# Decay and rate up-projections of a hybrid RWKV-7 / HGRN-2 layer: two products on 128 rows in place of three on 64

## The chip, the cores and the metric

The kernel runs on one core of a Trainium2 chip, as one launch. Its time is the device time in microseconds (us). Before the change it is 3080.24 us, the median of three runs (3078.0 to 3082.81). The engines are PE (matrix products, with weight loads, PEld, beside them), DVE (VectorE), ACT (ScalarE), POOL (GpSimd) and SP, which only issues DMAs. Each takes its own instructions in the order of the program.

## The reference

One layer on x [2048, 1024]. A projection u = x @ w_in feeds two branches. What the change touches is in the first:

```
u = u + (token_shift(u) - u) * mu
xw = u[..., C_WD:C_AD]        # 64 inputs of the decay
xa = u[..., C_AD:C_GD]        # 64 inputs of the rate
w_log = -softplus(-(w0 + tanh(xw) @ w_up)) - 0.5      # w_up [64, 512]
decay = exp(-exp(w_log))
a = sigmoid(a0 + xa @ a_up)                           # a_up [64, 512]
g = sigmoid(xg) @ g_up                                # 128 inputs
y = rwkv7_scan(r, decay, k, v, -kk, kk * a)
```

The second branch is a gated recurrence in chunks (HGRN-2, 4 heads). Both go through gates and an output matrix, then follow a layer norm, a routed mixture of 32 experts, a second layer norm and a gate on a side input. All of it is in float32.

## The kernel before

**Precision.** Products in the type fp32r are made exact enough by splitting both operands: `split` (lines 66 to 72) writes the high part by an ACT copy and the low part by a DVE subtraction. A product is then high x high, high x low and low x high.

**Phases.** The first phase (`phase_a`, to about 1640 us) computes the projection and both recurrences; then come the output products with gates (names pp, wab, gt), w_o with the first norm and the router, the experts, and the end. The first phase goes over four blocks of 512 tokens. A block has 46 projections `proj(ct)` of 128 columns, each of 24 products (lines 269 to 271: eight parts of the features, three products each), four head pairs of the first branch and four heads of the second. Projection 12 holds the 64 decay inputs on partitions 0 to 63 and the 64 rate inputs on 64 to 127; projection 13 the 128 gate inputs; 0 to 11 r, k and v; 14 to 29 the heads of the second branch; 30 to 45 the gates. `prep` makes projections 12 and 13 and splits their results into lh, ll (decay and rate) and gh, gl (gate).

**The up-projections.** Per head pair (128 of 512 columns) `s1a` calls `lora` twice. With r the rows 0 to 63 for the decay (pw), 64 to 127 for the rate (pa), it issues three products that contract over 64 partitions:

```
PE.matmul(o, wh[r, c], ah[r], start=True, stop=False)     # L333
PE.matmul(o, wh[r, c], al[r], start=False, stop=False)    # L334
PE.matmul(o, wl[r, c], ah[r], start=False, stop=True)     # L335
```

The gate's up-projection (pg) uses the same function with all 128 rows.

**The first branch.** `g1` forms the chunk products (pA, line 420); DVE masks them (A, line 425), and the lower triangles go to DRAM (Lsc) and back (Lt). `inv` inverts 32x32 blocks on DVE in 31 steps (lines 455 and 457), and the result goes through DRAM (Msc) into MI. `g2` makes further operands (pB, pV); `ops` combines (p, line 534); `chain` runs the state through 8 chunks of a head pair (py lines 571 and 572, pt 578, Sbd, ST). `hgrn` is the second branch: levels of masked products (g, line 649; kc, att), then transposes (tk, tv), po and pS.

**What sets the order.** The generators of a block are woven by weights, which gives the program its first order; then the tile framework reorders each engine's instructions by its own timing model (`schedule_with_timeline_sim=True`). So any edit can give another order, on all engines. Tiles lie on two stacks of pools in SBUF, and a later phase's tile waits for the earlier ones in its place. `tt` gives a ring of 4 scratch tiles, weights of a projection a ring of 3.

Of the kernel before, what the change touches and what calls it, by code (L numbers as in the profile page):

```python
# [10 lines left out]
F32 = mybir.dt.float32  # L11
F32R = mybir.dt.float32r
# [10 lines left out]
T = 2048  # L23
# [25 lines left out]
def hybrid_kernel(ctx, tc, x, p, w_in, rw_mu, rw_w0, rw_w_up, rw_a0, rw_a_up, rw_g_up, rw_k_k, rw_k_a,  # L49
# [66 lines left out]
    def phase_a(pool, lpool):  # L116
# [51 lines left out]
        def load_x(b, xh, xl, tags):  # L168
            """x^T of block b, split: a step for each 128 of its features"""
# [53 lines left out]
        plb = cp.tile([128, 4], F32, name="plb")      # lb + (1-lb)/2  # L223
# [10 lines left out]
        hlb = cp.tile([128, 4], F32, name="hlb")      # (1-lb)/2  # L234
# [5 lines left out]
        # loras  # L240
        wua_h = cp.tile([128, 512], F32R, name="wua_h")
        wua_l = cp.tile([128, 512], F32R, name="wua_l")
# [3 lines left out]
        ltmp = tt("ltmp")  # L246
        nc.sync.dma_start(ltmp[0:64], rw_w_up[0])
        nc.sync.dma_start(ltmp[64:128], rw_a_up[0])
        split(wua_h, wua_l, ltmp)
# [31 lines left out]
        def turned2(dst, src, g4):  # L281
            """block-diagonal form of four chunks, columns (half, head, 32), the halves changed over in odd chunks"""
            for h in range(2):
                r = slice(64 * h, 64 * h + 64)
                for u in range(2):
                    i_ = src[r, 4 * g4 + u:4 * g4 + 4:2, :].rearrange("q c (a t) -> q c a t", a=2)
                    yield (dst[r].rearrange("q c (a x t) -> q c a x t", a=2, x=2)[:, u::2, :, h, :],
                           i_[:, :, ::-1, :] if u else i_)
# [3 lines left out]
        def block(b):  # L292
# [19 lines left out]
            def prep():  # L312
                if b == 0:
                    bt["xh"], bt["xl"] = x0
# [1 line left out]
                lh = bt["lh"] = ev.tile([128, 512], F32R, tag="lh", name=f"lh{b}")  # L316
                ll = bt["ll"] = ev.tile([128, 512], F32R, tag="ll", name=f"ll{b}")
# [4 lines left out]
                split(lh, ll, u)  # L322
# [7 lines left out]
            def lora(wh, wl, ah, al, r, hp, name, tag="rw"):  # L330
                o = bank(tag, 2, name)
                c = slice(128 * hp, 128 * hp + 128)
                PE.matmul(o, wh[r, c], ah[r], start=True, stop=False)  # L333
                PE.matmul(o, wh[r, c], al[r], start=False, stop=False)  # L334
                PE.matmul(o, wl[r, c], ah[r], start=False, stop=True)  # L335
                return o

            def rstd_bcast(sq, ones, n, eps, opm, name, tag):
                """[128, 512] of rows' (max(sum, eps) or sum + eps)^-1/2, broadcast over the summed rows, in PSUM."""
# [17 lines left out]
            def s1a(hp, ukv, st):  # L357
# [3 lines left out]
                pw = lora(wua_h, wua_l, bt["lh"], bt["ll"], slice(0, 64), hp, "pw" + n)  # L361
# [16 lines left out]
                pa = lora(wua_h, wua_l, bt["lh"], bt["ll"], slice(64, 128), hp, "pa" + n)  # L378
# [30 lines left out]
            def g1(hp, st):  # L409
                """a^T (b, k, I) of the chunks; L to DRAM"""  # L410
# [21 lines left out]
            def inv(hp, st):  # L432
                """inverse of the 32x32 diagonal blocks of I - L"""
# [8 lines left out]
                # partition (g, blk): row r is row 4r+g of the identity  # L442
# [24 lines left out]
            def g2(hp, st):  # L467
                """b^T, k^T with (r, I); the centred v; block-diagonal forms"""
# [50 lines left out]
            def ops(hp, st):  # L519
                """chunk operators"""  # L520
# [20 lines left out]
                # (I - L)^-1 by halves of 32 tokens: a pair of chunks at a time  # L541
# [23 lines left out]
            def chain(hp, st):  # L565
# [22 lines left out]
                pg = lora(gu_h, gu_l, bt["gh"], bt["gl"], slice(0, 128), hp, "pg" + n, "ch")  # L588
# [6 lines left out]
            def hgrn(h, hook=None):  # L595
# [11 lines left out]
                V.scalar_tensor_tensor(q, q, 1.0, pq, op0=ALU.add, op1=ALU.mult)     # 2 silu(q)  # L607
# [106 lines left out]
            def next_x():  # L714
                """loads x, and has a step of its turn into x^T for each of the last ones of the block before"""
# [31 lines left out]
        cen = cp.tile([128, 128], F32, name="cen")    # I - ones/64 within each head  # L747
# [6 lines left out]
        # tokens of a chunk's a and b on partitions (half, head, 32): the halves change places in odd chunks  # L754
        strictP = cp.tile([128, 2, 64], F32, name="strictP")  # (., parity, s): s < t
        strictH = cp.tile([128, 2, 2, 64], F32, name="strictH")  # the same, one head's rows
        inclP = cp.tile([128, 2, 64], F32, name="inclP")      # (., parity, t): t >= s
        inclT = cp.tile([128, 64], F32, name="inclT")         # partition (h,s), col t: t >= s
# [23 lines left out]
        # HGRN: odd chunks hold k and v backwards, so that a level's earlier halves of an even and of an odd chunk  # L782
        # lie on complementary positions.  Masks: position s, (chunk, later half's t)
        hm = cp.tile([128, 7, 128], U8, name="hm")
        hmf = tt("hmf")[:, 0:128]
        for lv in range(7):
# [3 lines left out]
            for u, sg in ((0, 1), (1, -1)):  # L790
                # keep 2h*b <= s < 2h*b + h, where s is the position or 127 minus it
# [6 lines left out]
        # persistent tiles with fixed zero or identity parts  # L798
# [60 lines left out]
    def ln_rows(pl, s, n, bufs=2):  # L859
        """mean and rstd of the rows of s [128, D] -> (rstd, -mean * rstd)"""  # L860
# [73 lines left out]
    def phase_b2(pool, outp, mg, last):  # L934
# [33 lines left out]
        def first(d, io, oh, name):  # L968
            """one-hot of the first place where d (value minus the maximum) is 0"""
# [8 lines left out]
        def route(b, lg):  # L978
# [32 lines left out]
            # exp(d) = (1 + tanh(d/2)) / (1 - tanh(d/2))  # L1011
# [91 lines left out]
    def pe_setup(hold, tmp):  # L1103
        """p @ w_pe, row tile by row tile, into pe_d: the first NPE tiles wait for the end of the experts"""
# [632 lines left out]
```

## Time and profile before

| | |
|---|---|
| median of three runs | 3080.24 us (3078.0 to 3082.81) |
| span of the profiled execution, its only time | 3081.2 us |
| PE busy | 2993.2 us, 97% |
| PEld busy (beside PE) | 2571.2 us, 83% |
| DVE busy | 2130.2 us, 69% |
| ACT busy | 1554.2 us, 50% |
| POOL busy | 541.5 us, 18% |

The profile is of one execution. Busy times of PE are modelled and overlap by a part of each product, so the step from one start to the next says what a product takes of the stream. The clock of PE has two levels, and a stretch shows their mean (1.00 is full). A row of waits gives who waited, for whom, the us in total, how often, and the longest.

### The profile page before, as it was taken

To read this page: it belongs to the slowest core of one execution; us is meant where nothing else is said; L and a number is where in the kernel's file an instruction comes from. 1 tells how busy PE (TensorE), PEld (TensorE's weight loads), DVE (VectorE), ACT (ScalarE), POOL (GpSimd) and SP (SyncE) were. 2 spreads that over 40 slices of the span, in tenths; PEclk is the share of its full clock that TensorE was granted. 3 is DMA by queue.
4 is the path that set the end of the run, shared out by engine and by line. 5 is a ranking of instruction groups with operands and counts; after the bars stand their busy time and mean duration, and the time that the engine had idled before them with its cause. 6 is when DMAs were issued, how large, how long until landed. Compare 5 with 4: busy or idle time off the path is not lost.

```text
span 3081.2 us, 50028 instructions
## 1 busy us (share of the span) xinstructions
PE 2993.2 (97%) x17080; PEld 2571.2 (83%) x17080; DVE 2130.2 (69%) x4827; ACT 1554.2 (50%) x3119; POOL 541.5 (18%) x827
## 2 busy tenths in 40 slices
PE   8999999999999999999988999998999999999799
PEld 6888888888888888888877999987888888887687
DVE  5777768777777767777678777754545555655785
ACT  5555555555655556555534434333545555555442
POOL 4111112211112111212113011121111111112200
PEclk9999999999999999999999999999999999999899
DMA  4333323333233242323335333239889999996661
GB/s 119 96 88 101 105 76 99 88 87 113 83 95 85 87 119 83 91 81 85 87 100 178 110 101 111 89 130 366 292 294 327 315 333 332 338 337 232 233 225 68
DMA packets 438135, 491.41 MB, mean 159 GB/s; under 512 B 91334, under 2 KB 310470, under 8 KB 437878
## 3 DMA queue, kind: packets, MB, share of 16 engines
q1 hardware_dynamic: 424566, 445.45, 44.9%
q0 software_dynamic: 13312, 42.74, 3.8%
q8 instruction: 136, 2.23, 0.3%
q14 instruction: 121, 0.99, 0.1%
HBM read 417.66 MB, written 70.42 MB: 158 GB/s over the span
## 4 chain that ended last, share of the span: by engine, by line
PE 85%; DVE 6%; DMA 4%; issue 2%; SPq 1%; ACT 1%; POOL 0%; POOLq 0%; DVEq 0%; ACTq 0%
PE pp L269 10%; PE pp L271 10%; PE pp L270 10%; PE py L1339 7%; PE w1p L1394 4%; PE p L534 3%; PE w3p L1394 3%; PE po L1064 2%; PE po L1062 2%; PE po L1063 2%; PE pg L1555 2%; PE pg L1556 2%; PE pp L923 2%; PE pp L922 2%; PE pp L921 2%
## 5 line engine op out<-in xcount | busy, mean ns | idle before, releaser
L69 DVE TENSOR_TENSOR lw<-w,hw 128x1024 fp32r<-128x1024 f32 x256 | 308.9, 1222 | 207.6 <-ACT hw L67 205.6
L67 ACT ACTIVATE hw<-w 128x1024 fp32r<-128x1024 f32 x256 | 267.5, 1056 | 117.1 <-PE py L1339 64.3
L455 DVE TENSOR_TENSOR pr<-M,Lt 128x2 f32<-128x2 f32 (+30 forms) x496 | 169.5, 342 | 35.2 <-POOL Lt L441 24.8
L921 PE MATMUL pp<-yh,wh 128*128 128x256 f32 x512 | 146.5, 287 | 7.2 <-DVE gt L924 7.2
L923 PE MATMUL pp<-yh,wl 128*128 128x256 f32 x512 | 146.2, 286 | 3.7 <-DVE wl L69 3.7
L922 PE MATMUL pp<-yl,wh 128*128 128x256 f32 x512 | 146.9, 288 | 0.0
L1394 PE MATMUL w1p<-xT,w 128*128 128x152 f32 (+5 forms) x1024 | 143.7, 297 | 0.7 <-ACT xT L1311 0.7
L67 ACT ACTIVATE wh<-wab 128x512 fp32r<-128x512 f32 x128 | 80.1, 629 | 123.3 <-PE pp L922 121.2
L1394 PEld LDWEIGHTS w1p<-xT,w 128*128 128x128 f32 x1024 | 139.1, 192 | 2.6 <-ACT xT L1311 0.9
L1394 PE MATMUL w3p<-xT,w 128*128 128x152 f32 (+5 forms) x1024 | 136.3, 294 | 0.0
L1394 PEld LDWEIGHTS w3p<-xT,w 128*128 128x128 f32 x1024 | 134.5, 190 | 0.0
L457 DVE TENSOR_REDUCE M<-pr 128x1 f32<-128x2 f32 (+30 forms) x496 | 126.1, 254 | 10.5
L1351 POOL DMA_INDIRECT ybuf<-y,it x48 | 62.2, 1297 | 297.0 <-ACT y L1349 225.7
L921 PEld LDWEIGHTS pp<-yh,wh 128*128 128x128 f32 x512 | 98.4, 193 | 10.7 <-issue 7.0
L1318 DVE SCALAR_TENSOR_TENSOR u<-t,w3p 128x512 f32<-128x512 f32 (+6 forms) x48 | 26.1, 543 | 113.4 <-PE w3p L1394 83.3
L923 PEld LDWEIGHTS pp<-yh,wl 128*128 128x128 f32 x512 | 98.5, 193 | 6.5 <-DVE wl L69 5.6
L1265 POOL DMA_INDIRECT xg<-x_d,it x48 | 52.4, 1092 | 288.9 <-DMA it<-tokbuf 284.0
L69 DVE TENSOR_TENSOR wl<-wab,wh 128x512 fp32r<-128x512 f32 x124 | 89.4, 722 | 19.7 <-ACT wh L67 18.3
L1339 PE MATMUL py<-hw,hTl 128*128 128x512 f32 x256 | 102.2, 399 | 0.0
L1339 PE MATMUL py<-lw,hTh 128*128 128x512 f32 x256 | 101.8, 397 | 0.0
L1062 PE MATMUL po<-woh,mh 128*128 128x512 f32 x256 | 101.5, 397 | 0.0
L1063 PE MATMUL po<-woh,ml 128*128 128x512 f32 x256 | 101.2, 395 | 0.0
(1044 smaller groups left out, 9422.1 us busy)
## 6 DMA issues: line engine op xcount, KB each, us to landing
w<-in_w_dram SPq DMA_DIRECT2D x384, 512.0 KB
gt_d<-gt SPq DMA_DIRECT2D x64, 256.0 KB
gt<-gt_d SPq DMA_DIRECT2D x64, 256.0 KB
yg<-ybuf SPq DMA_DIRECT2D x32, 512.0 KB
xr<-in_x_dram SPq DMA_DIRECT2D x32, 256.0 KB
Lt<-Lsc SPq DMA_DIRECT2D x64, 128.0 KB
xr<-in_x_dram SPq DMA_DIRECT2D x16, 512.0 KB
x_d<-s SPq DMA_DIRECT2D x16, 512.0 KB
```

The lines of the kernel that those rows point to most:

```text
L67: a = S.activation(hi, src, AF.Copy, **({} if scale is None else {"scale": scale}))
L69: v = (G if pool else V).tensor_tensor(lo, src, hi.bitcast(F32), op=ALU.subtract)
L269: PE.matmul(o, wh[:, i % 4, :], xh, start=(i == 0), stop=False)
L270: PE.matmul(o, wh[:, i % 4, :], xl, start=False, stop=False)
L271: PE.matmul(o, wl[:, i % 4, :], xh, start=False, stop=(i == n - 1))
L455: V.tensor_tensor(pr[:, r0:, 0:w], M[:, r0:, j:32], lt[:, None, :].to_broadcast([128, 8 - r0, w]), op=ALU.mult)
L921: PE.matmul(pp[:, u, :], w[u][0][:, k, :], yh[i], start=(k == 0), stop=False)
L922: PE.matmul(pp[:, u, :], w[u][0][:, k, :], yl[i], start=False, stop=False)
L923: PE.matmul(pp[:, u, :], w[u][1][:, k, :], yh[i], start=False, stop=(k == 3))
L1062: PE.matmul(po, mh[:, tsl], woh[k][:, cs], start=(k == 0), stop=False)
L1339: PE.matmul(py[c][0:n], h[:, j, :], st["w2s", j][w][:, cs], start=(j == 0 and i == 0), stop=(j == 3 and i == len(seq) - 1))
L1394: PE.matmul(ph[nm][j // 2][:, j % 2, 0:cap], st[nm, k // 2][:, k % 2, 128 * j:128 * j + 128], xT[:, k, 0:cap], start=(k == 0 and j % 2 == ...
```

## The change

The weights of the decay and of the rate get a tile each (high and low part), with the 64 rows of the matrix on partitions 0 to 63 and once more on 64 to 127. The 64 inputs of the decay become one tile lw: the high part on partitions 0 to 63, the low part on 64 to 127. For the rate, la has the low part on 0 to 63 and the high part on 64 to 127. One product over 128 rows with the high weights then adds high x high and high x low; a second with the low weights adds low x high, and low x low, which before was left out. The gate keeps its three products. The per-partition area for GpSimd's DMA descriptors at the foot of SBUF goes to 8192 bytes, from the build's default of 16384; the two more weight tiles take 4096.

```diff
-        wua_h = cp.tile([128, 512], F32R, name="wua_h")
-        wua_l = cp.tile([128, 512], F32R, name="wua_l")
+        wua = {c: [cp.tile([128, 512], F32R, name=f"w{c}_{q}") for q in "hl"] for c in "wa"}
...
-        ltmp = tt("ltmp")
-        nc.sync.dma_start(ltmp[0:64], rw_w_up[0])
-        nc.sync.dma_start(ltmp[64:128], rw_a_up[0])
-        split(wua_h, wua_l, ltmp)
+        for c, up in (("w", rw_w_up), ("a", rw_a_up)):
+            ltmp = tt("ltmp" + c)
+            for r in (slice(0, 64), slice(64, 128)):
+                nc.sync.dma_start(ltmp[r], up[0])
+            split(*wua[c], ltmp)
...
-                lh = bt["lh"] = ev.tile([128, 512], F32R, tag="lh", name=f"lh{b}")
-                ll = bt["ll"] = ev.tile([128, 512], F32R, tag="ll", name=f"ll{b}")
+                lw = bt["lw"] = ev.tile([128, 512], F32R, tag="lw", name=f"lw{b}")
+                la = bt["la"] = ev.tile([128, 512], F32R, tag="la", name=f"la{b}")
...
                 S.activation(u[0:64], u[0:64], AF.Tanh)
-                split(lh, ll, u)
+                r0, r1 = slice(0, 64), slice(64, 128)
+                split(lw[r0], lw[r1], u[r0])
+                split(la[r1], la[r0], u[r1])
...
-            def lora(wh, wl, ah, al, r, hp, name, tag="rw"):
+            def lora(wh, wl, xs, hp, name, tag="rw"):
                 o = bank(tag, 2, name)
                 c = slice(128 * hp, 128 * hp + 128)
-                PE.matmul(o, wh[r, c], ah[r], start=True, stop=False)
-                PE.matmul(o, wh[r, c], al[r], start=False, stop=False)
-                PE.matmul(o, wl[r, c], ah[r], start=False, stop=True)
+                for i, a in enumerate(xs):
+                    PE.matmul(o, wh[:, c], a, start=(i == 0), stop=False)
+                PE.matmul(o, wl[:, c], xs[0], start=False, stop=True)
                 return o
...
-                pw = lora(wua_h, wua_l, bt["lh"], bt["ll"], slice(0, 64), hp, "pw" + n)
+                pw = lora(*wua["w"], (bt["lw"],), hp, "pw" + n)
...
-                pa = lora(wua_h, wua_l, bt["lh"], bt["ll"], slice(64, 128), hp, "pa" + n)
+                pa = lora(*wua["a"], (bt["la"],), hp, "pa" + n)
...
-                pg = lora(gu_h, gu_l, bt["gh"], bt["gl"], slice(0, 128), hp, "pg" + n, "ch")
+                pg = lora(gu_h, gu_l, (bt["gh"], bt["gl"]), hp, "pg" + n, "ch")
...
-    nc = _bacc.Bacc("TRN2", target_bir_lowering=False, num_devices=1)
+    nc = _bacc.Bacc("TRN2", target_bir_lowering=False, num_devices=1, dynamic_dma_scratch_size=8192)
```

The scheduler gives most instructions of the first phase another place; behind it the order is all but the same. Lines of the changed kernel are up to five higher. Three places follow.

ACT at the start of the program; m is the scaled projection 12, u its shifted form, w_13h the weights of projection 13. Before:

```order
L67 ACTIVATE wua_h<-ltmp 128x512
L305 ACTIVATE m_12_302<-pp_12_277,mu 128x512
L67 ACTIVATE gu_h<-ltmp_261 128x512
L67 ACTIVATE w_13h_313<-w_13r_311 128x512
L321 ACTIVATE u_12_305<-u_12_305 64x512
L67 ACTIVATE w_13h_319<-w_13r_317 128x512
L67 ACTIVATE lh_273<-u_12_305 128x512
```

And now:

```order
L67 ACTIVATE ww_h<-ltmpw 128x512
L307 ACTIVATE m_12_309<-pp_12_284,mu 128x512
L67 ACTIVATE wa_h<-ltmpa 128x512
L67 ACTIVATE gu_h<-ltmp_268 128x512
L324 ACTIVATE u_12_312<-u_12_312 64x512
L67 ACTIVATE la_281<-u_12_312 64x512
L67 ACTIVATE w_13h_322<-w_13r_320 128x512
L67 ACTIVATE lw_280<-u_12_312 64x512
L67 ACTIVATE w_13h_328<-w_13r_326 128x512
```

The first half of projection 13's weights has six copies ahead of it from the up-projections' weights on, before three.

PE in the first head pair of block 1, from the end of projection 8 to the start of projection 14. Before:

```order
L271 MATMUL pp_8_4654<-xh_7_4240,w_8l_4651 128x512
L333 MATMUL pw_0_4737<-lh_4281,wua_h 128x512
L334 MATMUL pw_0_4737<-ll_4282,wua_h 128x512
L335 MATMUL pw_0_4737<-lh_4281,wua_l 128x512
L333 MATMUL pa_0_4759<-lh_4281,wua_h 128x512
L334 MATMUL pa_0_4759<-ll_4282,wua_h 128x512
L335 MATMUL pa_0_4759<-lh_4281,wua_l 128x512
L269 MATMUL pp_14_4960<-xh_0_4156,w_14h_4950 128x512
```

And now:

```order
L273 MATMUL pp_8_4657<-xh_7_4241,w_8l_4654 128x512
L339 MATMUL pw_0_4740<-lw_4282,ww_h 128x512
L340 MATMUL pw_0_4740<-lw_4282,ww_l 128x512
L339 MATMUL pa_0_4761<-la_4283,wa_h 128x512
L340 MATMUL pa_0_4761<-la_4283,wa_l 128x512
L271 MATMUL pp_14_4961<-xh_0_4157,w_14h_4951 128x512
```

Six products of 64 rows give way to four of 128 rows; nothing else stands between the projections.

SP at the end of the phase; Msc and MI are the last inverse's way through DRAM, wab the output weights, gt_0 to gt_2 the gates of the next phase. Before:

```order
L702 DMA gt_d_78<-gt_14_17200 128x512
L461 DMA Msc_3_16724<-M_3_16731 256x1x32 x4
L464 DMA MI_484<-Msc_3_16724 32x4x32 x2
L464 DMA MI_486<-Msc_3_16724 32x4x32 x2
L464 DMA MI_484<-Msc_3_16724 32x4x32 x2
L464 DMA MI_486<-Msc_3_16724 32x4x32 x2
L886 DMA wab_17622<-in_w_a_out_dram 128x4x256
L886 DMA wab_17622<-in_w_b_out_dram 128x4x256
L702 DMA gt_d_78<-gt_15_17400 128x512
```

And now:

```order
L707 DMA gt_d_78<-gt_14_17183 128x512
L891 DMA wab_17605<-in_w_a_out_dram 128x4x256
L891 DMA wab_17605<-in_w_b_out_dram 128x4x256
L707 DMA gt_d_78<-gt_15_17383 128x512
L921 DMA gt_0_17673<-gt_d_75 128x2x256
L921 DMA gt_1_17723<-gt_d_75 128x2x256
L921 DMA gt_2_17776<-gt_d_75 128x2x256
L466 DMA Msc_3_16707<-M_3_16714 256x1x32 x4
L469 DMA MI_493<-Msc_3_16707 32x4x32 x2
```

The stores and loads of the last inverse go behind two loads of output weights, one store and three loads of gates.

## Rows read from the trace of the kernel before

**Rows 1.** the page: the span, and each engine's busy us, share, instructions

```profile
span 3081.2 us, 50028 instructions
...
PE 2993.2 (97%) x17080; PEld 2571.2 (83%) x17080; DVE 2130.2 (69%) x4827; ACT 1554.2 (50%) x3119; POOL 541.5 (18%) x827
```

**Rows 2.** windows: us, each engine's busy us (instructions), clock, DMA share, GB/s

```profile
270.00:660.00 390.00, 388.29 (x2208) 333.78 (x2208) 294.14 (x769) 218.24 (x517) 73.98 (x132) 1.00 0.33 93
...
1440.00:1640.00 200.00, 184.11 (x1112) 160.48 (x1110) 148.27 (x408) 97.01 (x247) 32.43 (x47) 0.96 0.33 99
```

**Rows 3.** timeline of PE: start us, us, engine, line, operation, tiles, shape, count

```profile
1481.41 0.39 PE L270 MATMUL pp<-xl,w_28h 128*128 128x512 f32 x1
1481.64 0.39 PE L271 MATMUL pp<-xh,w_28l 128*128 128x512 f32 x1
1481.96 0.50 PE L333 MATMUL pw<-lh,wua_h 64*128 64x512 f32 x1
1482.30 0.39 PE L334 MATMUL pw<-ll,wua_h 64*128 64x512 f32 x1
...
1483.18 0.39 PE L270 MATMUL pp<-xl,w_40h 128*128 128x512 f32 x1
```

**Rows 4.** timeline of PE, first head pair of block 1

```profile
422.42 0.40 PE L271 MATMUL pp<-xh,w_8l 128*128 128x512 f32 x1
422.75 0.49 PE L333 MATMUL pw<-lh,wua_h 64*128 64x512 f32 x1
422.76 0.49 PE L333 MATMUL pa<-lh,wua_h 64*128 64x512 f32 x1
...
423.99 0.40 PE L270 MATMUL pp<-xl,w_14h 128*128 128x512 f32 x1
```

**Rows 5.** timeline of PE, a group with a state product inside

```profile
1489.33 0.49 PE L572 MATMUL py<-GP,ST 128*128 128x128 f32 x2
1489.74 0.50 PE L334 MATMUL pa<-ll,wua_h 64*128 64x512 f32 x1
```

**Rows 6.** one line: operation, tiles, count: duration ns min/median/max, first and last start

```profile
L333 PE MATMUL pw<-lh,wua_h x16: 491/496/497, 28.2 to 1482.0; 64*128 64x512 f32 x16
```

**Rows 7.** the start: timeline, wait (us, times, longest), and window of the clock

```profile
17.62 0.58 SPq L248 DMA_DIRECT2D ltmp<-in_rw_a_up_dram  x1
...
22.18 0.62 ACT L67 ACTIVATE w_13h<-w_13r 128x512 fp32r<-128x512 f32 x1
...
PE pp L269 <- ACT w_13h L67: 3.8, 1, 3.8
...
22.80:26.90 4.10, 3.80 (x9) 2.78 (x10) 3.01 (x5) 2.19 (x5) 3.84 (x10) 0.58 0.46 127
```

**Rows 8.** the tiles of the split inputs: count and duration ns

```profile
L67 ACT ACTIVATE lh<-u x4: 612/618/619, 24.5 to 1191.7; 128x512 fp32r<-128x512 f32 x4
L69 DVE TENSOR_TENSOR ll<-u,lh x4: 684/684/723, 25.3 to 1192.4; 128x512 fp32r<-128x512 f32 x4
```

**Rows 9.** end of the phase: timeline of DVE and PE, windows

```profile
1527.15 0.68 DVE L425 TENSOR_TENSOR A<-A,strictP 128x512 f32<-128x512 f32 x1
...
1598.17 1.13 PE L534 MATMUL p<-GP,C 128*128 128x128 f32 x8
1599.14 0.39 PE L679 MATMUL po<-q,HS 128*128 128x128 f32 x2
...
1527.00:1571.00 44.00, 43.48 (x279) 38.76 (x279) 36.63 (x111) 20.87 (x49) 7.14 (x11) 1.00 0.23 70
1571.00:1610.00 39.00, 30.10 (x203) 27.04 (x201) 26.76 (x75) 14.10 (x44) 5.76 (x5) 0.91 0.27 82
```

**Rows 10.** waits of SP and PE; a window of loaded DMA queues

```profile
SPq L886 <- DVE HS L682: 18.1, 1, 18.1
...
PE tr L1298 <- DMA xg<-x_d,it: 17.1, 7, 9.2
...
2070.00:2300.00 230.00, 214.73 (x1146) 186.61 (x1145) 109.43 (x151) 106.50 (x151) 34.62 (x38) 0.95 0.88 309
```

## Prediction

> **What bounds the kernel now.** I read the page first. TensorE (PE) is busy 97% of the 3081.2 us; VectorE (DVE), the next, 69% [rows 1]. Then the stretches. In the 390 us from 270 us on, a block's length, PE is busy 388.3 us at full clock, DVE 294 us [rows 2]: there PE's instruction stream is the time, and a product taken out of it is gained. From 1440 to 1640 us, the end of the first phase, PE is busy only 184 of 200 us at a clock of 0.96 [rows 2]: there a chain over several engines sets the end. Then, instruction by instruction, the up-projections that the change touches.
>
> Back-to-back projection products start 0.23 us apart; here the first half-height product starts 0.32 us after a projection, the second 0.34 us after the first, and from there to the second projection behind are 0.88 us [rows 3]. Busy durations (0.39 to 0.50 us) overlap, so I count starts. From 1481.64 to 1483.18 us are 1.54 us; two projections alone take 0.46, so these three products cost 1.08 us: 0.69 for three slots and 0.39 for going to 64 rows and back.
>
> **The change part by part.** *PE, removed.* There are 32 groups of three (16 for the decay [rows 6], as many for the rate). Going along the timeline I find 21 like [rows 3]: 21 x 1.08 = 22.7 us. In three, a state product stands between the first and second half product [rows 5], one change of height there and back more: 3 x (1.08 + 0.39) = 4.4 us. In the first head pair of blocks 1, 2 and 3 the decay's and the rate's products stand together and start 0.01 us apart, two at a time on different rows: 1.57 - 0.46 = 1.11 us for all six [rows 4], so 3.3 us. In block 0 the first two groups take four slots in three places: 4 x 0.23 + 3 x 0.39 = 2.1 us. Sum 32.5 us.
>
> *PE, added.* 64 full-height products of 512 columns. I take 0.23 us each, as the projections have with the same height, columns and type [rows 3]; none changes the height. 64 x 0.23 = 14.7 us. Bounds: 0.23 below, 0.34 above (the start that a first product costs there). PE's gain is 32.5 - 14.7 = 17.8 us, and 10.7 us at the upper bound.
>
> [...]
>
> *The split of the 64 inputs.* Per block one ACT copy of 0.62 us and one DVE subtraction of 0.68 us [rows 8] become two of each on 64 rows. I take the same duration per instruction, since the columns stay: 4 x 0.62 us more on ACT, 4 x 0.68 us more on DVE. Bounds: nothing if half the rows took half the time, 5.2 us if all of it lay on the path. In blocks 1 to 3 three projections (72 products of 0.23 us, 16.6 us) stand between the inputs' split and its first reader, so I take 0. Without that cover it is 1.3 us a block.
>
> *The start.* The small weights are loaded twice: two DMAs more, and one split more. PE then stands waiting for the split of projection 13's weights, 3.8 us [rows 7]. On SP two more issues of about 0.6 us lie ahead of that load; on ACT the order puts one more split of 0.62 us, the tanh and one copy of the inputs (taken at the same 0.62) ahead of it [rows 7]. So about 1.9 us later. PE runs at a mean clock of 0.58 in the 4.1 us behind its wait [rows 7]; a longer wait may hold that, so 1.3 to 3 us. I take +2.0. SP's queue has the loads of projection 0 and later behind, each 1.2 us later, all inside this.
>
> *The order.* In the first phase the tile scheduler laid all engines out anew; behind it nothing but names moves. In the stretch of a middle block PE idled 1.7 us of 390 [rows 2], so over the three blocks in front another order can hardly gain; I take 0, bounds -5 (three times 1.7) and +5. The end of block 3 is different. There the last inversion of the small blocks runs from the mask of A at 1527.15 us to the product that needs it and the state chain, at 1598.17 us [rows 9]. In the new order that mask's PE products (pA of head pair 3) have 165 projection products behind them in the phase and its successor's first part, in the old 184: 19 x 0.23 = 4.4 us of projections now stand ahead of it, and besides 24 passes of 128 columns of the recurrences, at 0.12 us (eight of them in 0.97 us [rows 9]) 2.9 us. So that chain starts about 7 us later than the saved products alone would give: +7.0. But the stretch has slack: from 1527 to 1610 us DVE is busy 36.6 of 44 and 26.8 of 39 us, PE 43.5 and 30.1 at a clock of 0.91 in the second part [rows 9], so PE idles 9.4 us. In the new order the gated recurrence's products fill the time of the inversion, and after it only two of the eight steps of the chain of head pair 2 remain, before five. I take back about half of PE's idle time, -5.0; bounds 0 and -9.4.
>
> *The smaller descriptor area* (8192 bytes a partition) serves GpSimd's gathers and scatters. PE's waits for gathered rows are 17.1 us over seven times [rows 10]. No row shows GpSimd waiting for room, so I take 0; bounds 0 and +17 if these waits doubled.
>
> Sum: 3081.2 - 17.8 + 0 + 2.0 + 7.0 - 5.0 + 0 = 3067.4 us. The profiled execution's only time is its span, 1.0 us above the median of the three runs, 3080.24; so I forecast **3066 us**.
>
> **The rivals.** *A: the end of the phase keeps what PE gives.* Nothing of the idle time is refilled, and the stores of the inverse, now behind 1 MB of output weights and 0.75 MB of gates on SP (third order block), land later: 1.75 MB at the 309 GB/s of a loaded stretch [rows 10] is 5.7 us. 3081.2 - 17.8 + 2 + 7 + 5.7 - 1.0 = 3077. For it: DVE's share there, and that nothing is queued ahead of these stores in the old order. Against it: the loads may have ended before the last step of the inversion. Chance 0.17.
>
> *B: slower, the queue of SP.* SP issues in order. One load of output weights waited 18.1 us for DVE's state update [rows 10]. If the load that now stands ahead of the inverse's stores has such a wait, the inverse is late by it, and a loss of clock behind the wait as at the start (4.1 us at 0.58 [rows 7], 1.7 us): 3081.2 - 17.8 + 2 + 7 + 18.1 + 1.7 - 1.0 = 3091. It decides from about 13 us of wait on. Against it: that tile lies where block 3's x^T was, read for the last time by the last projection, before the inversion ends; it is the second weight tile that lies over the states. Chance 0.06, in which I put the gathers (+17) too.
>
> *C: full-height products cost more than they look.* At 0.34 us each: 3081.2 - 10.7 + 2 + 7 - 5 - 1 = 3073.5. For it: each group's first product may wait for its inputs' rows. Against: the projections' 0.23 behind each other. Chance 0.07.
>
> *D: the end gains more.* The new order refills all 9.4 us and starts the chain no later than the saving gives: 3081.2 - 17.8 + 2 - 9.4 - 1 = 3055. Chance 0.10.
>
> **How the numbers follow.** The forecast has 0.60, with an own range of 3060 to 3073 from the start's and the end's bounds. About 0.2% (6 us) is what a measurement of this kernel can tell from no change. Faster takes the forecast, D and half of C and a little of A; the rest of A and C is the same; B is slower: 0.76, 0.18, 0.06. The range leaves out B, the far side of D and half of A: 3056 to 3078.
>
> **What would show it.** In the changed profile: two products of 128x512 per group, 0.23 us apart, with 0.23 us to the projections on either side (right), 0.32 or more (C). The wait of PE for projection 13's weights 1.5 to 2.5 us longer. The mask of A for the last head pair about 9 us earlier than 1527, the product behind the chain about 14 us earlier than 1598 (A: under 6; D: over 20). PE's waits for gathered rows unchanged. From the third phase on every stretch should be as long as before; if a stretch there moves by more than 2 us, the layout in memory or the descriptor area acts where I took nothing, and the forecast is wrong whatever its number.

## The result and the profile after

The changed kernel is slower: 3104.55 us (median of four runs, 3100.23 to 3108.13) against 3079.46 us in the same comparison, a ratio of 1.0074 [1.0059, 1.0089]. A second measurement, used below as the control, gave 3103.71 us, ratio 1.0079 [1.0066, 1.0092]. The forecast of 3066 us missed in sign: it said faster, and it lies some 38 us too low, outside its range. Each kernel is compared by ratio with the kernel before measured beside it, whose median went from 3079.46 to 3082.86 us. Executions at a lower granted clock are left out of all medians and ratios (two of the eight with the old order below, 3459 and 4851 us at 0.81 and 0.57 in place of 0.986).

The page after, which answers to [rows 1]:

```profile
span 3103.0 us, 49966 instructions
...
PE 2990.1 (96%) x17048; PEld 2576.9 (83%) x17048; DVE 2133.9 (69%) x4832; ACT 1557.9 (50%) x3124; POOL 530.9 (17%) x827
```

PE has the 32 products fewer that the change promised, yet the span is 21.8 us longer. The windows after (length, busy us of PE, PEld, DVE, ACT, POOL with instructions, clock, DMA share, GB/s), the first and last answering to [rows 2]:

```profile
270.00:660.00 390.00, 387.13 (x2202) 334.94 (x2201) 293.70 (x768) 218.99 (x518) 69.52 (x132) 1.00 0.33 94
660.00:1050.00 390.00, 383.90 (x2170) 331.86 (x2169) 288.47 (x735) 214.40 (x506) 64.62 (x127) 0.99 0.32 92
1050.00:1440.00 390.00, 383.01 (x2181) 330.57 (x2181) 295.12 (x766) 215.03 (x505) 71.94 (x131) 1.00 0.32 91
1440.00:1640.00 200.00, 183.71 (x1056) 158.60 (x1054) 136.58 (x387) 91.55 (x241) 29.24 (x43) 0.94 0.33 97
```

The same two middle windows of the kernel before:

```profile
660.00:1050.00 390.00, 388.70 (x2206) 334.06 (x2205) 291.58 (x758) 214.87 (x509) 70.68 (x129) 1.00 0.33 93
1050.00:1440.00 390.00, 387.87 (x2200) 333.07 (x2200) 290.83 (x747) 218.16 (x514) 71.21 (x129) 1.00 0.33 93
```

PE's idle time there rises from 1.3 to 6.1 us and from 2.1 to 7.0 us: the loss lies inside the blocks, where the prediction took the order for neutral. In time, the start of the first phase's last transpose of the state (`pt<-ident,Sbd`), here called the phase's end, moves by +14.6 us, before to after:

```profile
1627.89 0.27 PE L578 MATMUL pt<-ident,Sbd 128*128 128x128 f32 x1
```

```profile
1642.53 0.27 PE L583 MATMUL pt<-ident,Sbd 128*128 128x128 f32 x1
```

Each trace is of one execution; traces of kernels with the same order and products put this end up to 1.9 us apart. Behind it the span is 1453.3 us before and 1460.5 after, +7.2 (7.1 in the control's trace); 3.2 of that is one wait behind the experts (below). The rest is no more than this stretch moves anyway: over all traces it takes 1445.9 to 1463.0 us.

What the products do was foreseen, all but a small part. A group after (timeline of PE: start, us, engine, line, operation, tiles, shape, count), which answers to [rows 3]:

```profile
1503.33 0.47 PE L339 MATMUL pw<-lw,ww_h 128*128 128x512 f32 x1
1503.64 0.39 PE L340 MATMUL pw<-lw,ww_l 128*128 128x512 f32 x1
1503.87 0.39 PE L273 MATMUL pp<-xh,w_17l 128*128 128x512 f32 x1
```

Its starts are 0.31 and 0.23 us apart. The mean from a product's start to the next start is 0.251 us over all 64, 16.1 us in all for the 14.7 forecast (0.241 and 15.4 in the old order of the next section): 15 of the 64 take 0.31 or 0.32, the others 0.23 or 0.24.

To add this up, each matmul's distance to the next start is valued at the median that the same pair of neighbouring shapes has over the kernels compared. That is "undisturbed steps". The rest of a distance, its excess, is put down to waits of 0.25 us and more, to stretches of half clock (granted 0.50; the traces of before and after record no clock but this and 1.00), or to shorter waits. In the first phase, before to after:

| | before | after | old order (next section) |
|---|---|---|---|
| undisturbed steps, us | 1530.2 | 1511.3 | 1514.0 |
| waits of 0.25 us and more | 31.7 | 50.7 | 35.1 |
| half clock without a wait | 8.4 | 16.9 | 11.1 |
| shorter waits | 4.5 | 7.4 | 5.0 |

The steps shrink by 18.9 us, and by 16.2 in the old order; the forecast was 17.8. How neighbours are grouped moves these values by a us or more. Waits, half clock and short waits give back 30.4; the other 3 us of the 14.6 lie in steps without a wait.

### The profile page after: what moved, and what is told of

Same layout as the page of the kernel before. It is cut to its first block, busy times and chain, and to the rows that moved or that the text cites. A ratio compares the mean times of both kernels' runs of the same rounds, so it can differ in the third digit from the quotient of the medians.

```text
span 3103.0 us, 49966 instructions
## 1 busy us (share of the span) xinstructions
PE 2990.1 (96%) x17048; PEld 2576.9 (83%) x17048; DVE 2133.9 (69%) x4832; ACT 1557.9 (50%) x3124; POOL 530.9 (17%) x827
## 3 DMA queue, kind: packets, MB, share of 16 engines
q8 instruction: 136, 2.23, 0.3%
## 5 line engine op out<-in xcount | busy, mean ns | idle before, releaser
L69 DVE TENSOR_TENSOR wl<-wab,wh 128x512 fp32r<-128x512 f32 x124 | 89.5, 723 | 19.6 <-ACT wh L67 18.8
```

Source lines behind the costliest of these rows:

```text
L69: v = (G if pool else V).tensor_tensor(lo, src, hi.bitcast(F32), op=ALU.subtract)
```

## The experiments

An experiment that pins an order adds, between consecutive instructions of each engine, a dependency without a semaphore, so that the scheduler has one order to choose. The few instructions that only one of two kernels has stand behind those that they resemble; nothing else differs (shortened):

```
+    for e, seq in order_of_the_other_kernel.items():
+        for p, q in zip(seq, seq[1:]):
+            tc.add_manual_dep(q, p.name, NoSync, reason="order")
```

Pinning by itself costs nothing: the kernel before, pinned to its own order (with the smaller area and two spare tiles, `p6_layout` below), has a ratio of 0.9995.

**Order and descriptor area.** First: the changed kernel, each engine's first phase in the order of before.

> The changed kernel (two full-height products, second set of small weights, smaller descriptor area), with every engine's order in the first phase fixed to that of the kernel before: each instruction is queued behind the one that stood ahead of it there, without a wait; the extra split and loads stand right behind the ones that they resemble. Theory ORDER (the products save what they should, about 18 us, and the new order of the first phase loses about 33): the wait behind the first phase (gates, at 1647.0 us before and 1661.6 after) comes at 1629 to 1634, and the time is 3062 to 3072 us, by whether the later phases keep the 7 us that they lost in the changed kernel. Rival PRODUCTS (the stacked products or the layout in memory cost what was lost, whatever the order): the wait at 1650 or later, the time at 3085 or more.

Measured: 3070.29 us, ratio 0.9965 [0.9946, 0.9984]; the phase ends 12.0 us ahead of before. That end, its products and its middle blocks (timelines and windows of this run):

```profile
1615.92 0.27 PE L583 MATMUL pt<-ident,Sbd 128*128 128x128 f32 x1
```

```profile
1466.25 0.40 PE L273 MATMUL pp<-xh,w_28l 128*128 128x512 f32 x1
1466.48 0.39 PE L339 MATMUL pw<-lw,ww_h 128*128 128x512 f32 x1
1466.71 0.40 PE L340 MATMUL pw<-lw,ww_l 128*128 128x512 f32 x1
1466.94 0.39 PE L271 MATMUL pp<-xh,w_40h 128*128 128x512 f32 x1
```

```profile
660.00:1050.00 390.00, 387.64 (x2218) 336.80 (x2217) 295.60 (x770) 218.62 (x517) 72.02 (x132) 1.00 0.33 93
1050.00:1440.00 390.00, 388.00 (x2215) 336.78 (x2215) 295.87 (x770) 220.00 (x519) 71.38 (x132) 1.00 0.33 93
```

0.23 us on either side of each product, and PE as full as before: in a fixed order the change is a gain.

Second: the kernel before with the smaller descriptor area alone.

```
-    nc = _bacc.Bacc("TRN2", ..., num_devices=1)
+    nc = _bacc.Bacc("TRN2", ..., num_devices=1, dynamic_dma_scratch_size=8192)
```

> The kernel before with the smaller descriptor area (8192 bytes) alone; its order is the same on every engine. Theory AREA (the smaller area, or the addresses that it shifts, makes the 7 us that the changed kernel lost behind the first phase): 3084 to 3090 us, with a wait for y rows of about 5 us near 2850 us as in the changed kernel. Rival (it does nothing; these 7 us come from the two added weight tiles or from when the phase starts): 3079 to 3082.

3081.78 us, 1.0002 [0.9989, 1.0016]: it does nothing.

Third: the products of before, in the order of the changed kernel.

> The kernel before (three half-height products, its own memory layout and descriptor area), with every engine's order in the first phase fixed to that of the changed kernel. Theory ORDER: the new order alone loses about 30 us in the first phase, so its end comes 30 to 35 us later than before and the time is 3105 to 3118 us, slower than the changed kernel. Rival PRODUCTS: no loss without the stacked products, 3078 to 3085.

3116.87 us, 1.0123 [1.0105, 1.0142]. The phase's end, and PE's middle blocks with the changed kernel's holes but without its products:

```profile
1656.78 0.27 PE L578 MATMUL pt<-ident,Sbd 128*128 128x128 f32 x1
```

```profile
660.00:1050.00 390.00, 382.98 (x2163) 328.59 (x2162) 287.17 (x736) 212.43 (x504) 67.38 (x128) 1.00 0.32 90
1050.00:1440.00 390.00, 381.37 (x2116) 324.90 (x2115) 284.08 (x746) 204.67 (x481) 68.28 (x123) 0.99 0.32 91
```

With these runs the four corners stand. End of the phase, us:

| | order of before | order of after | order's cost |
|---|---|---|---|
| products of before | 1627.9 | 1656.8 | +28.9 |
| products of after | 1615.9 | 1642.5 | +26.6 |
| gain of the products | -12.0 | -14.3 | |

By the ratios the order costs more, about 34 us on the new products (1.0074 against 0.9965) and 38 on the old (1.0123). What lies beyond the phase's 27 to 29 us falls behind its end or between single executions; no run here separates the two.

**Other orders by a neutral knob.** One weight of the planner is changed, which moves the order and nothing else; one such run each for 33 in place of 32 (`WN`) and 41 in place of 40 (`WC`), on the kernel before:

```
-        WI, WG, WC, WH, WN = 42.0, 12.0, 40.0, 32.0, 32.0
+        WI, WG, WC, WH, WN = 42.0, 12.0, 40.0, 32.0, 33.0    # or WC 41.0
```

> The kernel before with one weight of the weave in the first phase (of the stream that prepares the next head pair) at 33 instead of 32: the same instructions, in another order on all engines. Theory ORDER (the order of before is a good one among many, and another costs tens of us): 3090 to 3115 us. Rival (orders differ by less than 5 us; the new order of the change is bad for a reason of its own): 3075 to 3086.

3114.46 us, 1.0102 [1.0084, 1.012]: a step of 3% in one weight costs 32 us.

> The kernel before with another weight of the weave changed in the first phase (that of the operators and state chain of the head pair behind) to 41 from 40: the same instructions, another order on all engines. Theory DRAW (the order of before is a good draw and nearly any other costs 15 to 40 us, whatever causes it): 3095 to 3120 us. Rival (p4's 32 us are special to its weight): 3078 to 3090 us.

3090.03 us, 1.0021 [1.0008, 1.0034]: 7 us, between the two ranges and in neither; that nearly any other order costs 15 us or more is not so. And the changed kernel, in its own scheduler's order, with 41 and with 33, and its control:

> The changed kernel with the weave's weight of the operators and state chain at 41 instead of 40, as in p10: another order with the changed products, nothing pinned. Theory DRAW (each weight gives an order with its own loss, and p10's weight gave before a loss of 6 to 15 us and not 28): 3070 to 3090 us, faster than the changed kernel by 15 us or more. Rival (the changed products are slow in any order but the old one): 3098 to 3112 us.

> The changed kernel with the weight WN 33 for 32, which changes the order of the first phase and nothing else; on the kernel before the same weight cost 31.6 us. DRAW (every order that the list scheduler finds is one of many, and its time doesn't follow from the weight): anything from 3065 to 3105 us, not 31.6 us above the changed kernel; its first phase ends where the waits and half-clock stretches of its own order put it, and its stream of undisturbed steps is again about 19 us shorter than before's. WEIGHT (this weight is a worse rule as such): some 25 to 35 us above the changed kernel, 3129 to 3139.

> The changed kernel itself, beside the others on this chip, as the value that p9, p11 and p12 are compared with: by both theories 1.006 to 1.009 times the kernel before.

3083.82 us, 1.0013 [1.0002, 1.0024]; 3110.29 us, 1.010 [1.008, 1.012]; and 3103.71 us. So the same weight 33 that cost 32 us on the old products costs some 7 us on the new ones (the range given to that draw ended at 3105, 5 us too low), and 41, which cost the old ones 7 us, gives the new ones 20. The time doesn't follow the weight. Among three orders that the scheduler found for each kernel, 3084 to 3110 us after and about 3081 to 3114 before, the one that before happened to have is the fastest of all six, with the costlier products.

**Which wait.** In block 2 the order of after loses most. VectorE's timeline there, with the idle time ahead of an instruction and its releaser in brackets:

```profile
952.84 0.35 DVE L584 TENSOR_SCALAR ST<-pt,wc 128x128 f32<-128x128 f32 x1 [1.80 <-PE pt L583]
...
955.40 0.16 DVE L460 TENSOR_TENSOR pr<-M,Lt 128x2 f32<-128x2 f32 x1 [2.21 <-POOL Lt L446]
...
957.00 0.34 DVE L687 SCALAR_TENSOR_TENSOR HS<-HS,T,pS 128x128 f32<-128x128 f32 x1
```

and PE's answer, with the window behind it:

```profile
957.39 0.79 PE L684 MATMUL po<-q,HS 128*128 128x128 f32 x2 [3.24 <-DVE HS L687]
```

```profile
956.70:963.50 6.80, 6.11 (x20) 5.37 (x21) 4.77 (x20) 3.48 (x9) 0.55 (x2) 0.50 0.14 39
```

The first step of an inversion (`pr`) waits 2.21 us for Lt, which comes back through memory. The state update HS, which PE needs, stands behind it in VectorE's one queue. PE waits 3.24 us, and from the last 0.7 us of that wait on its granted clock is 0.50 for 6.8 us. PE's waits of this kind between 30 and 1500 us (who waited, for whom, us in total, times, longest), before and after:

```profile
PE po L679 <- DVE HS L682: 0.4, 1, 0.4
```

```profile
PE po L684 <- DVE HS L687: 6.4, 4, 3.2
```

The next run keeps all orders of the changed kernel and moves two HS updates of the first head, in blocks 1 and 2, ahead of that step.

> The changed kernel in its own order, with two instructions of VectorE moved: the third state update (HS) of the gated recurrence of block 1's and block 2's first head goes ahead of the first step of the inversion, where it stood five to six places behind it (the trace: that step waits 2.0 and 2.2 us for its matrix from memory, and TensorE waits 1.5 us at 558.2 and 3.2 us at 954.2 us for the two updates). Theory QUEUE (the order loses where VectorE, in order, waits for a transfer ahead of something that TensorE needs): these two waits go, with the half-clock stretch at 956.7 to 963.5 us, and the time falls 4 to 8 us below the changed kernel's (to 3097 to 3101 us at the changed kernel's 3104.5). Rival DIFFUSE (the next waits take their place): 0 to 2 us.

3093.74 us, 1.0032 [1.0021, 1.0044], against 1.0079 for the control: about 14 us less. Only 8.1 us of that lie in the phase (its end is at 1634.39), which is the upper end of the 4 to 8 forecast; the other 6 lie behind it, where nothing was changed and traces differ by more. The update and its reader now:

```profile
951.00 0.35 DVE L687 SCALAR_TENSOR_TENSOR HS<-HS,T,pS 128x128 f32<-128x128 f32 x1 [0.55 <-PE pS L686]
```

```profile
951.40 0.49 PE L684 MATMUL po<-q,HS 128*128 128x128 f32 x2
```

Then nine more instructions of VectorE moved in the same way, each picked from a wait in the trace.

> p9_two_updates with nine VectorE instructions more moved ahead, each to where its inputs were ready by the trace of p9: one more HS update (TensorE waited 1.0 us for it at 1046.4), three q updates of the gated recurrence (waits 1.0, 0.9 and 0.7 us), the low part of x^T (1.1), a blended input that holds a PSUM bank (1.7), two state operators (1.8 and 0.5), a state copy (0.5); 9.2 us of waits in all. They stood behind steps of the inversion and weight splits that were not late themselves. Theory QUEUE (what is left of the loss in blocks 0 to 3 is VectorE's sequence too): half or more comes back, the time is 4 to 9 us below p9. Rival PILE (VectorE is full in these stretches, so that whatever is moved back is late next): 0 to 3 us.

3101.78 us, 1.0069 [1.0054, 1.0084]: the gain is gone. Most of the chosen waits went, and others came up that with two moves were 0.4 us or nothing (PE's waits from 900 to 1500 us: total, times, longest):

```profile
PE py L577 <- DVE ST L584: 1.9, 2, 1.7
PE gn_0b L359 <- ACT gn_0e L356: 1.7, 1, 1.7
PE pp L271 <- ACT vv L607: 1.7, 1, 1.7
PE pV L510 <- ACT YH L506: 1.7, 1, 1.7
```

Was the first success luck? The order with weight 41 has the same fault in a purer form, six times in blocks 1 to 3. PE's waits from 30 to 1500 us there, and the worst place:

```profile
PE po L684 <- DVE HS L687: 13.6, 6, 4.4
```

```profile
1348.80 0.16 DVE L460 TENSOR_TENSOR pr<-M,Lt 128x2 f32<-128x2 f32 x1 [4.97 <-POOL Lt L446]
...
1349.97 0.33 DVE L687 SCALAR_TENSOR_TENSOR HS<-HS,T,pS 128x128 f32<-128x128 f32 x1
```

These six updates, and nothing else, are moved by one rule laid down beforehand:

```
+ block 1..3, head 0: third HS<-HS,T,pS directly behind the second
+ block 1..3, head 1: third HS<-HS,T,pS directly behind the ST before it
```

> The changed kernel with the weight 41 (3083.8 us, first phase 1632.6), all orders kept, but six updates HS<-HS,T,pS on VectorE are moved: in blocks 1 to 3 the third one of the first head directly behind the second, and the third one of the second head directly behind the last ST before it, so that none stands behind a step of the inversion that waits for Lt. PE waited 13.6 us for these six. QUEUE (the update held in VectorE's queue is what the new order costs): all six waits go, most of the 13.6 us comes back, the first phase ends at 1619 to 1626 and the median falls by 6 to 13 us, to 3071 to 3078. PILE (PE has other waits right behind, and the moved update makes VectorE wait for pS in its place): the six waits shrink but others grow, the first phase ends at 1630 to 1634 and the median moves by 3 us at most.

3074.10 us, 0.9977 [0.9967, 0.9986], from 1.0013 with the updates where they were: about 11 us. The phase ends at 1617.46, 15.1 us earlier. PE's waits for HS and the same place now:

```profile
PE po L684 <- DVE HS L687: 0.7, 3, 0.2
```

```profile
1336.84 0.35 DVE L687 SCALAR_TENSOR_TENSOR HS<-HS,T,pS 128x128 f32<-128x128 f32 x1 [1.92 <-PE pS L686]
1338.85 0.16 DVE L460 TENSOR_TENSOR pr<-M,Lt 128x2 f32<-128x2 f32 x1 [1.66 <-POOL Lt L446]
```

VectorE now waits 1.92 us for pS first and 1.66 for Lt after it, instead of 4.97 for Lt alone, and PE's wait there falls from 4.43 to 0.22 us. In PE's sum the long waits fall by 11.6 us (44.6 to 33.0) and the half clock by 7.3 (15.8 to 8.5). That settles the mechanism for this order: the update held in VectorE's queue. It does not settle it for after's own order, where it stands for 8 us of about 27.

**The start, the third tile, the layout.** The old order again, with the loads and splits of projection 13's weights moved ahead of the inputs' at the start.

> The run p1_old_order (changed products, order of before) with one move more at the start: projection 13's two weight loads go on SP right behind the load of w0h, ahead of ten small vectors and the small weights, and their splits on ACT and DVE go right behind projection 12's. Theory START (the added loads and splits cost about 2 us of p1 because they stand ahead of projection 13's weights, and the whole wait there, 6.0 us, comes from that queue): PE's wait for w_13h falls from 6.0 to under 1.5 us, the first product of projection 13 comes at 19 to 20.5 us and not 24.9, and the time is 5 to 8 us below p1_old_order. Rival (the small weights, now later, hold the first decay product as long): the gain is under 2 us.

3073.68 us, 0.9971 [0.996, 0.9983], no better than 0.9965. The wait was exchanged, not removed: the first product of projection 13 starts at 21.43 instead of 24.93 us, but the decay's product then waits for its inputs (PE's waits, columns as above):

```profile
PE pw L339 <- DVE lw L69: 4.1, 1, 4.1
```

and the phase ends only 1.0 us earlier (1614.9).

Behind the experts, PE's products p @ w_pe go by tiles of 128 rows, and the third tile starts with one long wait, before and after:

```profile
2851.67 0.51 PE L1142 MATMUL pe<-wpeh,ph 128*128 128x512 f32 x1 [2.23 <-DVE pl L69]
```

```profile
2870.69 0.79 PE L1147 MATMUL pe<-wpeh,ph 128*128 128x512 f32 x1 [5.42 <-DMA yg<-ybuf]
```

The releaser in brackets is not the cause: the product does not read yg. In front of this tile the program has a loop, `tc.For_i(0, n, 1)`, for tokens that an expert had no room for; in these traces no instruction of its body runs. What grew is the longest of the three branches that PE's sequencer runs for it (duration in ns, min/median/max), before and after:

```profile
L1468 PEldq COMPARE_BRANCH  x3: 101/190/410, 2847.2 to 2851.4; - x3
```

```profile
L1473 PEldq COMPARE_BRANCH  x3: 101/193/3584, 2863.0 to 2870.4; - x3
```

That is 3.17 us of the 3.19 by which the wait grew.

Is it memory layout? Before's order, the smaller area, and two spare tiles, cleared and read by nobody, as large as the new weights' share:

```
+        for q in "hl":
+            spare = cp.tile([128, 512], F32, name=f"spare_{q}")
+            G.memset(spare, 0.0)
```

> The kernel before, its order kept, with the memory layout of the changed one: the smaller descriptor area and two more tiles of 128x512 where the changed kernel has its added weight tiles (only cleared, by two GpSimd instructions at the start). It has the product count of before. Theory LAYOUT (addresses make the later phases slower): the third-tile wait of the p @ w_pe products near 2850 us is 5.4 us as in the changed kernel and p1_old_order, and the time is 3084 to 3090 us. Rival COUNT (32 products fewer ahead of it move that place in TensorE's program, and its weight load waits there for nothing the trace names): the wait stays 2.2 us as in before, p2 and p3, and the time is 3078 to 3083 us.

3081.28 us, 0.9995 [0.9983, 1.0006], with the wait still short:

```profile
PE pe L1145 <- DVE pl L69: 2.2, 1, 2.2
```

Is it the number of instructions ahead? The old-order kernel with 32 tiny products, which do nothing for the output, inside PE's wait at the start. The trace has two PE products for each (64, `fill<-ones`), so that PE's count is 17112, 32 above before's and not equal to it:

```
+        fill = bank("rw", 2, "fill")
+        for i in range(32):
+            PE.matmul(fill[0:2, 0:2], ones128, ones128, start=True, stop=True)
```

> p1_old_order with 32 products of 2x2 more on TensorE, put where it waits for projection 13's weights at the start, so that as many products as in before stand ahead of the later phases. Theory COUNT (the wait of 5.4 us at the third tile of p @ w_pe comes from where that product stands in TensorE's program): the wait falls back to 2.2 us, with a code packet of TensorE's queue 5 us or more ahead of its end and not inside it; the time is about 3 us below p1_old_order. Rival: the wait stays 5.4 us.

3068.12 us, 0.9967 [0.9954, 0.998]. The ratio is that of the old order alone (0.9965), so the 3 us that were expected do not show in the time. But the wait is short again, and so is the branch:

```profile
PE pe L1150 <- ACT ph L67: 2.6, 2, 2.1
```

```profile
L1476 PEldq COMPARE_BRANCH  x3: 101/187/327, 2832.0 to 2836.1; - x3
```

So the number of PE instructions ahead decides. In the nine kernels with 17048 products the wait is 5.3 to 5.6 us and the branch 3.42 to 3.76; in the seven with 17080 or 17112 they are 2.1 to 2.2 and 0.33 to 0.41. In each of the nine, a packet of an instruction queue (q8 on the page: 136 packets, 2.23 MB, so 16 KB each) starts 0.95 to 0.98 us into the branch, and the branch ends 1.43 to 1.52 us after the packet's end. In each of the seven, the next packet starts only after the branch is over; in the run with the tiny products it still starts 0.46 us ahead of the wait's end, which its expectation had not foreseen. That this queue is PE's, and that PE waited for the code in the packet, is the author's inference from these times; no run shows either by itself.

Of the kernels run, the old order with the 32 tiny products has the lowest median, 3068.12 us; by the ratios it is level with the old order alone. Both beat the kernel before, by 0.3%, and the changed one.

## Why the prediction was wrong

**The products: right.** Forecast -17.8 us, undisturbed steps -18.9 in after and -16.2 in the old order. The 64 products cost 0.251 and 0.241 us each on the mean, not 0.34; rival C is out. The split of the inputs is right too: `lw<-u` on 64 rows takes 627 ns on ACT and 685 on DVE, as on 128 [rows 8].

**The order: the step that failed.** It said that "over the three blocks in front another order can hardly gain; I take 0, bounds -5 (three times 1.7) and +5", and took these bounds from PE's idle time before, 1.7 us of 390 [rows 2]. Small idle time bounds what another order can gain. It says nothing on what it can lose, and the upper bound of +5 was the gain's mirrored, with no row behind it. Measured for the whole phase: +26.6 us on the new products, +28.9 on the old. In the three blocks in front, 0 to 2, after loses 20.4 us more than the old order with the same products (table), where the bound was +5. By stage, PE's loss beyond undisturbed steps in the first phase:

| | start | block 0 | 1 | 2 | 3 | end | sum |
|---|---|---|---|---|---|---|---|
| before | 11.9 | 16.4 | 14.8 | 13.9 | 11.6 | 24.7 | 93.2 |
| old order, new products | 13.8 | 15.7 | 14.3 | 14.3 | 9.7 | 29.7 | 97.6 |
| after | 15.5 | 18.8 | 18.3 | 27.6 | 14.2 | 32.5 | 126.9 |
| weight 41, new products | 13.6 | 18.1 | 21.0 | 19.8 | 19.2 | 25.6 | 117.4 |
| the same, six updates moved | 13.7 | 17.2 | 17.0 | 15.9 | 13.5 | 25.1 | 102.3 |

After loses 33.7 us more than before, 22.2 of it in blocks 0 to 3. A wait was paid for twice in places: its own time, and half clock after it. In the order of weight 41 PE's three waits of 2.9 to 4.4 us for HS each came with 3.4 to 6.8 us at 0.50, from the end of the wait on.

**Rival B: right in sign, wrong in place.** It put the slower case on SP's queue and the inverse's stores at 0.06. What stood in a queue behind a waiting instruction was VectorE's state update behind the inversion's first step. The rows for it were in the old trace: `pr` waits up to 3.7 us for Lt there too (DVE's waits from 0 to 1640 us), but PE's waits for HS are 0.4 us in all:

```profile
DVE pr L455 <- POOL Lt L441: 24.8, 16, 3.7
```

**The end of block 3: not as forecast.** The mask of A and the product behind the chain, [rows 9] after and in the old order:

```profile
1540.05 0.69 DVE L430 TENSOR_TENSOR A<-A,strictP 128x512 f32<-128x512 f32 x1 [1.93 <-ACT A L76]
...
1610.75 1.06 PE L539 MATMUL p<-GP,C 128*128 128x128 f32 x8
```

```profile
1510.10 0.68 DVE L430 TENSOR_TENSOR A<-A,strictP 128x512 f32<-128x512 f32 x1
...
1583.81 1.14 PE L539 MATMUL p<-GP,C 128*128 128x128 f32 x8
```

The prediction named 9 and 14 us earlier than before as its marks; after is 12.9 and 12.6 later. In the old order the mask comes 17.05 us earlier, the product 14.4 and the phase's end 12.0: the end gives back 5 us of what the products brought. The +7, a later start, can't be read apart from the losses ahead of it. The -5, a shorter way from the mask to the product, can: 71.0 us before, 70.7 after and 68.7 in the control, 0.3 to 2.3 us shorter.

**The start: right in the old order.** +2.0 forecast; the first product of projection 13 moves from 22.86 to 24.93 us there, +2.07, and the wait there grows from 3.8 to 6.0 us. In part this is luck: the same start is 23.7 us in the runs with the smaller area and with the spare tiles, whose products and order are before's, and against those it is +1.3. In after it is 26.08:

```profile
26.08 0.79 PE L271 MATMUL pp<-xh,w_13h 128*128 128x512 f32 x1 [7.09 <-ACT w_13h L67]
```

+3.2, with a clock of 0.50 in the 5.7 us behind it (before 0.58 [rows 7]). The share of the start's loss is 3.6 us (15.5 against 11.9).

**The descriptor area: right**, 0 by its own run, and PE's waits for gathered rows, 18.9 us in six against 17.1 in seven [rows 10], don't show it either. The mark for the later stretches (more than 2 us) was met by the third tile's wait, and the prediction read that mark wrongly: neither the layout nor the area made the wait, but the length of PE's program in front of a branch, which is not among its steps.

**What stays open.** Of the 26.6 us of after's order, two moved updates account for 8. The cause of the other 18 or so is not shown: apart from the start's, the waits left are under 2 us each, and nine moves at once removed most of those aimed at and made others. Of the 7.2 us behind the phase, 4 are unassigned.

## What to carry to other kernels

Where a scheduler sets the order, price an edit twice: with the old order held, and as a new draw of the order, whose spread is measured by turning a knob that should not matter (here 3081 to 3114 us for the old products). An engine at 99.6% busy [rows 2] has a lucky order to lose: its idle time bounds the gain of another one and not the loss. To look for the loss, look at the waits that its neighbours have under cover now, such as VectorE's waits for memory with harmless work queued behind them. A gain that a new order ate could be had back here by pinning the old order. Moving the one short instruction that the bounding engine needs ahead of the neighbour's waiting step worked for six updates in one order and for two in another, and failed when nine more were moved at once.

## What the runs showed of the hardware

A branch of PE's sequencer at a fixed place took 3.42 to 3.76 us in the nine kernels with 17048 PE products and 0.33 to 0.41 in the seven with 32 or 64 more, whatever the order or the layout; each of the nine had an instruction packet of 16 KB inside it. PE's granted clock was 1.00 in the 6.7 us from 950.0 us on in after, in which PE was busy 4.15 us and then waited; it fell in that wait of 3.24 us and stayed at 0.50 for 6.8 us, in which PE was busy 6.11.
